# Feed-forward of a hybrid recurrent step: the sample tokens of two or three tile pairs at once

## The chip, the cores and the metric

The kernel runs on one core of a Trainium2 chip: TensorE (matrix products), VectorE and GpSimd (elementwise), ScalarE (activations and copies), SyncE (here the queue that issues transfers), all beside each other. The metric is the device time of one execution in microseconds; the time that stands for a kernel is the median of its runs.

## The reference, cut to what matters

One layer of a decoder trunk for 512 prompt tokens and 8 sample sequences of 8 tokens each (576 token columns: `T`, of which `TP` = 512 are the prompt's). Four token mixers come first; the change is in what follows them:

```
xn2 = rmsnorm(x, norm2_w)
up, buf_ffn = causal_dwconv(xn2 @ ffn_up, buf_ffn, ffn_conv_w, ffn_conv_b)   # width 3; 1024 -> 5632
gate_h, val_h = split(up, 2)
x = x + (gelu(gate_h) * val_h) @ ffn_down                                    # 2816 -> 1024
```

```
def causal_dwconv(u, buf, w, b):
    full = concatenate([buf, u], axis=1)       # buf: the 2 inputs before the sequence
    out = b
    for j in range(3):
        out = out + full[:, j:j + n] * w[j]
    return out, full[:, n:]                    # the last 2 inputs are an output as well
```

For the prompt `buf` is zero; each sample sequence has its own.

## The kernel before

Channels lie on the 128 partitions and tokens along the columns. All products are float32 products made of three: a matrix is split into a high part (`whi`, `ah`: a copy by ScalarE with rounding) and a low part (`wlo`, `al`: the difference, by VectorE or GpSimd), and high x high, high x low and low x high are added up in PSUM.

In the feed-forward stage (`tail`) the 44 column tiles of `ffn_up` are worked off in 22 pairs: tile i of the gate half with tile 22 + i of the value half. `K.pair` forms each pair's products by Strassen's scheme in Winograd's form, with seven products in place of eight. For them it needs sums of weight tiles (L253, `wc` in SBUF and `mx` in PSUM), and seven sides that are split (L246 on ScalarE, L247 on VectorE or GpSimd by the list `STRASSEN`; `wsp` holds five high and five low tiles). The matmuls of a pair are L262: 7 products x 4 tiles x 3. Sums read in between are copied by ScalarE (L286), and the results are joined by VectorE and multiplied with each token's factor `rbc` (L677, L679, and GpSimd's L680) into `raw`, one 128 x 576 tile for each half.

`conv_tiles` then convolves each `raw` with `dwconv`. The prompt's 512 columns are accumulated in PSUM (`mx`): the last tap with the bias by ScalarE (L545), two taps by VectorE (L549). The samples' 64 columns are accumulated in SBUF (`accs`): ScalarE (L546), two short taps on VectorE (L556) and, by GpSimd, what the earlier inputs bring into the first two sums (L558, prepared once in `hist`, L584 to L592). GpSimd copies the last inputs aside for the state output (`fcs`, L686). The loop over the pairs takes gelu of the gate half and multiplies it with the value half, for the prompt and for the samples apart (L701, L702), and splits the joint tile `gl` into `ah` and `al` (L169, L170).

The pairs come in three chunks of 8, 7 and 7 (`CHUNKS`). After each chunk its rows of `ffn_down` are multiplied (L223 to L225, eight column tiles, two halves of 288 columns each, the second with the samples) and added to `x1` (L692). The last chunk's products are followed by the final norm and the outputs.

Nothing in this order is written by hand for an engine: a scheduler puts each engine's instructions into a queue by priorities and its own estimates when the kernel is built, so products with `ffn_down` and the next pair's weights can stand between each other. A queue runs in order.

## Time and profile before

| what | value |
|---|---|
| median of 3 runs | 1712.4 us (1711.94 to 1730.63) |
| span of the profiled execution | 1708.0 us |
| matmul busy, share of the span | 1623.3 us, 95% |
| VectorE busy | 1188.4 us, 70% |
| ScalarE busy | 694.8 us, 41% |
| GpSimd busy | 794.3 us, 47% |
| mean granted TensorE clock | 0.968 of full speed |

The span runs from the first to the last instruction of one execution; the time of a run is 4.4 us longer at the median, for what lies around it. Busy shares are means over stages that differ: the mixers fill most of the span, the stage with `ffn_up` and `ffn_down` lies from about 1276 to 1680 us. A matmul's recorded duration overlaps the next one's.

### The profile page before, as it was taken

How to read it: one execution, taken by the hardware profiler on the slowest of the kernel's cores; microseconds unless marked ns; L12 is line 12 of the kernel's file. 1: busy time of each engine (PE TensorE's matmuls, PEld its weight loads, DVE VectorE, ACT ScalarE, POOL GpSimd, SP SyncE). 2: the span in 40 equal slices, each digit the busy share in tenths (PEclk: the TensorE clock that was granted, in tenths of full speed). 3: DMA queues.
4: the chain of work that ended last, by engine and by line, in shares of the span. 5: the costliest groups of instructions: out<-in, count | busy, mean ns of one | idle time of the engine just before them, and what ended most of it. 6: DMA issues, size and time to landing. Idle time of an engine off the chain costs nothing. (4 is left out here: it accounts for less than half of the span.)

```text
span 1708.0 us, 32814 instructions
## 1 busy us (share of the span) xinstructions
PE 1623.3 (95%) x12200; PEld 1471.7 (86%) x12200; DVE 1188.4 (70%) x2584; ACT 694.8 (41%) x1489; POOL 794.3 (47%) x1013
## 2 busy tenths in 40 slices
PE   6989999999999998999999989999999999999997
PEld 5988888888888898878888888888998999989897
DVE  7888888777584288534338754686479965975985
ACT  6333323334332335323335443332356643653653
POOL 4645433435331356212235562275676734743750
PEclk9999889799899999989999999999999999999999
DMA  7545543453362456332336563665432332232232
GB/s 201 143 122 142 148 118 95 128 139 102 114 197 74 111 156 164 103 101 74 95 96 194 152 174 104 199 181 166 117 90 79 96 99 75 78 97 75 87 106 71
DMA packets 356452, 207.62 MB, mean 122 GB/s; under 512 B 110884, under 2 KB 328357, under 8 KB 356293
## 3 DMA queue, kind: packets, MB, share of 16 engines
q1 hardware_dynamic: 356293, 205.53, 43.0%
q8 instruction: 96, 1.57, 0.4%
q14 instruction: 63, 0.52, 0.1%
HBM read 151.54 MB, written 53.02 MB: 120 GB/s over the span
## 5 line engine op out<-in xcount | busy, mean ns | idle before, releaser
L223 PE MATMUL dn<-xh,whi 128*128 128x288 f32 x1392 | 429.3, 309 | 4.6 <-ACT st L414 1.9
L224 PE MATMUL dn<-xl,whi 128*128 128x288 f32 x1392 | 427.6, 307 | 2.0 <-DVE xl L170 1.7
L225 PE MATMUL dn<-xh,wlo 128*128 128x288 f32 x1392 | 427.2, 307 | 0.0
L223 PEld LDWEIGHTS dn<-xh,whi 128*128 128x128 f32 x1392 | 269.9, 194 | 19.4 <-issue 8.0
L224 PEld LDWEIGHTS dn<-xl,whi 128*128 128x128 f32 x1392 | 269.8, 194 | 14.6 <-issue 8.4
L225 PEld LDWEIGHTS dn<-xh,wlo 128*128 128x128 f32 x1392 | 270.1, 194 | 12.0 <-issue 7.8
L169 ACT CAST whi<-wraw 128x512 fp32r<-128x512 f32 (+1 forms) x278 | 173.5, 628 | 218.6 <-PE dn L224 209.6
L170 POOL TENSOR_TENSOR wlo<-wraw,whi 128x512 fp32r<-128x512 f32 x92 | 129.4, 1407 | 202.1 <-ACT whi L169 194.3
L170 DVE TENSOR_TENSOR wlo<-wraw,whi 128x512 fp32r<-128x512 f32 (+1 forms) x186 | 152.3, 819 | 72.1 <-ACT whi L169 60.8
L262 PE MATMUL dn<-big,whi 128*128 128x288 f32 x528 | 108.7, 298 | 8.7 <-ACT su L286 2.8
L247 POOL TENSOR_TENSOR wlo<-wraw,whi 128x512 fp32r<-128x512 f32 x66 | 90.1, 1372 | 48.1 <-ACT whi L246 48.0
L262 PE MATMUL dn<-xh,whi 128*128 128x288 f32 x352 | 104.8, 299 | 4.6 <-ACT whi L246 4.1
L223 PE MATMUL dn<-yh,whi 128*128 128x288 f32 x352 | 104.8, 304 | 3.0 <-ACT yh L166 1.9
L262 PE MATMUL dn<-xh,wlo 128*128 128x288 f32 x352 | 103.5, 298 | 4.4 <-POOL wlo L247 4.4
L224 PE MATMUL dn<-yl,whi 128*128 128x288 f32 x352 | 105.4, 300 | 1.1 <-DVE yl L167 1.1
L225 PE MATMUL dn<-yh,wlo 128*128 128x288 f32 x352 | 105.0, 299 | 0.0
L262 PE MATMUL dn<-xl,whi 128*128 128x288 f32 x352 | 103.5, 295 | 0.0
L223 PE MATMUL dn<-ah,whi 128*128 128x288 f32 (+2 forms) x324 | 95.1, 298 | 1.5 <-ACT ah L169 1.5
L224 PE MATMUL dn<-al,whi 128*128 128x288 f32 (+2 forms) x324 | 95.5, 296 | 0.6 <-DVE al L170 0.6
L262 PEld LDWEIGHTS dn<-big,whi 128*128 128x128 f32 x528 | 84.3, 188 | 12.5 <-ACT su L286 4.5
L225 PE MATMUL dn<-ah,wlo 128*128 128x288 f32 (+2 forms) x324 | 95.0, 295 | 0.0
L262 PE MATMUL dn<-big,wlo 128*128 128x288 f32 x264 | 77.7, 295 | 0.1
(743 smaller groups left out, 4093.1 us busy)
## 6 DMA issues: line engine op xcount, KB each, us to landing
wraw<-w_in SPq DMA_DIRECT2D x55, 512.0 KB
wraw<-ffn_up SPq DMA_DIRECT2D x44, 512.0 KB
wraw<-w_merge SPq DMA_DIRECT2D x32, 512.0 KB
gate<-gst SPq DMA_DIRECT2D x32, 288.0 KB
g<-gate SPq DMA_DIRECT2D x32, 288.0 KB
wraw<-ffn_down SPq DMA_DIRECT2D x16, 448.0 KB
pd_hg<-st SPq DMA_DIRECT2D x16, 288.0 KB
wraw<-w_br_ssd SPq DMA_DIRECT2D x8, 512.0 KB
```

The costliest lines, as they stand in the source:

```text
L169: nc.scalar.copy(out=hi, in_=src)
L170: lo_engine.tensor_tensor(out=lo, in0=src, in1=hi.bitcast(F32), op=ALU.subtract)
L223: nc.tensor.matmul(ps, wh, xh[k][:, sl], start=k == 0, stop=False)
L224: nc.tensor.matmul(ps, wh, xl[k][:, sl], start=False, stop=False)
L225: nc.tensor.matmul(ps, wl, xh[k][:, sl], start=False, stop=k == len(wt) - 1)
L247: TT[eng](out=lo, in0=src, in1=hi.bitcast(F32), op=ALU.subtract)
L262: nc.tensor.matmul(ps, wt[:, k], x, start=start and k == 0 and i == 0, stop=k == n - 1 and i == 2, skip_group_check=not start)
```

## The change

The samples leave `dwconv`. `conv_tiles` lets GpSimd copy the last two prompt columns and the 64 sample columns of each `raw` aside into `rs` (66 columns). The pairs of a chunk are grouped (3, 3, 2 or 3, 2, 2), and behind each group a new function `samples` does the convolution, gelu, product and split for its 4 or 6 tiles at once, with the taps' columns, the bias and the history put in a fitting order once, before the stage (`cols`, `hists`). `ah` and `al` become one tile each with room for eight. For the first two chunks the first two column tiles of `ffn_down` are taken together: first half of both, then second half of both. Comments were dropped from the whole file as well.

```
-def dwconv(K, acc, raw, hist, taps, w, bias, small, split=None):
+def dwconv(K, acc, raw, hist, taps, w, bias, small):
...
-    if split is None:
-        nc.scalar.activation(acc, raw, AF.Identity, bias=bias, scale=w(n - 1))
-    else:
-        nc.scalar.activation(acc, raw[:, :TP], AF.Identity, bias=bias, scale=w(n - 1))
-        nc.scalar.activation(split, raw[:, TP:], AF.Identity, bias=bias, scale=w(n - 1))
+    nc.scalar.activation(acc, raw if hist is not None else raw[:, :TP], AF.Identity, bias=bias, scale=w(n - 1))
     for j in range(n - 1):
...
+    if hist is None:
+        return
...
-    if split is not None:
-        for j in range(n - 1):
-            sh = n - 1 - j
-            nc.vector.scalar_tensor_tensor(out=av[:, :, sh:], in0=rv[:, :, :LS - sh], scalar=w(j), in1=av[:, :, sh:],
-                                           op0=ALU.mult, op1=ALU.add)
-        nc.gpsimd.tensor_tensor(out=av[:, :, :n - 1], in0=av[:, :, :n - 1], in1=hist, op=ALU.add)
-        return
...
     mul(hist[:, :, 1], hist[:, :, 1], w0)
...
+    hists = x1p.tile([P, 22, 2, NS, 2], F32, name="fhs")
+    cols = x1p.tile([P, 4, 22, 2], F32, name="fcol")
+    for h in range(2):
+        hc = slice(22 * h, 22 * h + 22)
+        for e_ in range(2):
+            nc.gpsimd.tensor_copy(out=hists[:, :, h, :, e_], in_=hist[:, :, e_, hc].rearrange("p b c -> p c b"))
+        for j in range(4):
+            nc.gpsimd.tensor_copy(out=cols[:, j, :, h], in_=K.vcs("ffn_conv_w", 44 * j, 44)[:, hc] if j < 3 else K.vcs("ffn_conv_b", 0, 44)[:, hc])
...
+    GROUPS = {8: (3, 3, 2), 7: (3, 2, 2)}
+
+    def conv_tiles(rs, *ms):
...
-        for m, raw in zip(ms, raws):
-            acc = K.ps(of="c"), fp.tile([P, T - TP], F32, tag="accs", bufs=3, name=K.n("accs"))
-            nc.gpsimd.tensor_copy(out=cs[:, :, :, m], in_=raw[:, TP - 2:].rearrange("p (b e) -> p b e", e=2)[:, 0::4, :])
-            dwconv(K, acc[0], raw, hist[:, :, :, m], 3, lambda j: K.vc("ffn_conv_w", j * 44 + m), K.vc("ffn_conv_b", m), fp, acc[1])
+        for h, (m, raw) in enumerate(zip(ms, raws)):
+            acc = K.ps(of="c")
+            nc.gpsimd.tensor_copy(out=rs[:, h], in_=raw[:, TP - 2:])
+            dwconv(K, acc, raw, None, 3, lambda j: K.vc("ffn_conv_w", j * 44 + m), K.vc("ffn_conv_b", m), fp)
             out.append(acc)
         return out
 
+    def samples(c, rs, ah, al):
...
+        n = rs.shape[1]
+        N = 2 * n
+        GT = nc.gpsimd.tensor_tensor
+        TT = nc.vector.tensor_tensor
+        r = rs.rearrange("p i h t -> p (i h) t")
+        for h in range(2):
+            m = slice(22 * h + c, 22 * h + c + n)
+            nc.gpsimd.tensor_copy(out=cs[:, 0, :, m].rearrange("p e c -> p c e"), in_=rs[:, :, h, :2])
+            for e_ in range(2):
+                nc.gpsimd.tensor_copy(out=cs[:, 1:, e_, m].rearrange("p b c -> p c b"), in_=rs[:, :, h, 2 + LS - 2 + e_::LS])
+        w = [cols[:, j, c:c + n].rearrange("p c h -> p (c h)").unsqueeze(2) for j in range(4)]
+        acc = fp.tile([P, 6, T - TP], F32, tag="sacc", bufs=2, name=K.n("sacc"))[:, :N]
+        GT(out=acc, in0=r[:, :, 2:], in1=w[2].to_broadcast([P, N, T - TP]), op=ALU.mult)
+        GT(out=acc, in0=acc, in1=w[3].to_broadcast([P, N, T - TP]), op=ALU.add)
+        av = acc.rearrange("p m (b t) -> p m b t", t=LS)
+        rv = r[:, :, 2:].rearrange("p m (b t) -> p m b t", t=LS)
+        ts = []
+        for j, sh in ((1, 1), (0, 2)):
+            t = fp.tile([P, 6, NS, LS], F32, tag="stap", bufs=2, name=K.n("stap"))[:, :N, :, :LS - sh]
+            TT(out=t, in0=rv[:, :, :, :LS - sh], in1=w[j].unsqueeze(3).to_broadcast([P, N, NS, LS - sh]), op=ALU.mult)
+            ts.append((sh, t))
+        GT(out=av[:, :, :, :2], in0=av[:, :, :, :2], in1=hists[:, c:c + n].rearrange("p c h b e -> p (c h) b e"), op=ALU.add)
+        for sh, t in ts:
+            TT(out=av[:, :, :, sh:], in0=av[:, :, :, sh:], in1=t, op=ALU.add)
+        a = acc.rearrange("p (i h) t -> p i h t", h=2)
+        g = fp.tile([P, 3, T - TP], F32, tag="sgl", bufs=2, name=K.n("sgl"))[:, :n]
+        nc.scalar.activation(g, a[:, :, 0], AF.Gelu_apprx_tanh)
+        TT(out=g, in0=g, in1=a[:, :, 1], op=ALU.mult)
+        K.split(ah, al, g, nc.vector)
+
...
     for k0, n in CHUNKS:
-        ah = [fp.tile([P, T], F32R, tag=f"ah{k}", name=K.n("ah")) for k in range(n)]
-        al = [fp.tile([P, T], F32R, tag=f"al{k}", name=K.n("al")) for k in range(n)]
-        for i in range(n):
-            accs = conv_tiles(k0 + i, 22 + k0 + i)
-            gl = fp.tile([P, T], F32, tag="gl", bufs=2, name=K.n("gl"))
-            for sl, a0, a1 in zip((slice(0, TP), slice(TP, T)), *accs):
-                nc.scalar.activation(gl[:, sl], a0, AF.Gelu_apprx_tanh)
-                nc.vector.tensor_tensor(out=gl[:, sl], in0=a1, in1=gl[:, sl], op=ALU.mult)
-            K.split(ah[i], al[i], gl, nc.vector)
...
+        hl = [fp.tile([P, 8, T], F32R, tag=t, name=K.n(t))[:, :n] for t in ("ah", "al")]
+        ah, al = ([t[:, k] for k in range(n)] for t in hl)
+        i = 0
+        for size in GROUPS[n]:
+            rs = fp.tile([P, 3, 2, T - TP + 2], F32, tag="rs", bufs=2, name=K.n("rs"))[:, :size]
+            for a in range(size):
+                a0, a1 = conv_tiles(rs[:, a], k0 + i, 22 + k0 + i)
+                gl = fp.tile([P, TP], F32, tag="gl", bufs=2, name=K.n("gl"))
+                nc.scalar.activation(gl, a0, AF.Gelu_apprx_tanh)
+                nc.vector.tensor_tensor(out=gl, in0=a1, in1=gl, op=ALU.mult)
+                K.split(ah[i][:, :TP], al[i][:, :TP], gl, nc.vector)
+                i += 1
+            samples(k0 + i - size, rs, *(t[:, i - size:i, TP:] for t in hl))
         if k0 + n < 22:
-            for m in K.dense(down, k0, n, 0, 8, ah, al, evac):
...
+            wt = [K.weights(down, k0, n, m * P) for m in range(2)]
+            for j in range(2):
+                for m in range(2):
+                    K.part(wt[m], slice(j * H2, (j + 1) * H2), ah, al, m, evac)
+            for m in K.dense(down, k0, n, 2 * P, 6, ah, al, lambda m, sl, ps: evac(m + 2, sl, ps)):
                 pass
```

## Rows read from the trace of the kernel before

**Rows 1.** The page: span, and busy time of each engine.

```profile
span 1708.0 us, 32814 instructions
...
PE 1623.3 (95%) x12200; PEld 1471.7 (86%) x12200; DVE 1188.4 (70%) x2584; ACT 694.8 (41%) x1489; POOL 794.3 (47%) x1013
```

**Rows 2.** Stretches: length, busy us (x instructions) of PE, PEld, DVE, ACT, POOL, clock, DMA.

```profile
1275.70:1377.40 101.70, 96.00 (x682) 91.28 (x682) 100.31 (x180) 66.37 (x140) 72.82 (x84) 1.00 0.30 85
1377.40:1427.80 50.40, 50.40 (x382) 50.40 (x381) 24.99 (x46) 14.43 (x25) 11.02 (x12) 1.00 0.28 81
1427.80:1516.00 88.20, 82.17 (x602) 80.03 (x601) 80.46 (x138) 54.13 (x111) 62.50 (x71) 1.00 0.30 88
...
1560.80:1650.70 89.90, 83.86 (x615) 81.66 (x614) 82.21 (x142) 55.72 (x114) 63.99 (x74) 1.00 0.30 86
...
1295.00:1377.40 82.40, 79.08 (x568) 75.75 (x567) 81.86 (x149) 55.22 (x116) 60.77 (x76) 1.00 0.32 92
1441.00:1516.00 75.00, 69.84 (x511) 67.94 (x511) 72.84 (x127) 48.06 (x99) 54.67 (x64) 1.00 0.31 89
1574.00:1650.00 76.00, 70.83 (x519) 68.86 (x518) 73.74 (x129) 49.05 (x101) 55.40 (x66) 1.00 0.30 88
```

**Rows 3.** Who waited for whom from 1275 to 1651 us: total, times, longest.

```profile
ACT whi L246 <- DVE mx L253: 20.3, 18, 2.2
...
ACT whi L246 <- DVE wc L253: 15.1, 14, 1.8
...
PE dn L262 <- ACT whi L246: 5.9, 10, 1.0
...
PE dn L262 <- POOL wlo L247: 4.4, 5, 1.2
```

**Rows 4.** One pair in order of time, VectorE, and a row of GpSimd: start, us.

```profile
1331.92 0.67 DVE L702 TENSOR_TENSOR gl<-mx,gl 128x512 f32<-128x512 f32 x1
...
1335.17 0.56 DVE L556 SCALAR_TENSOR_TENSOR accs<-raw,vecs,accs 128x48 f32<-128x48 f32 x2
...
1335.76 2.57 POOL L247 TENSOR_TENSOR wlo<-wraw,whi 128x512 fp32r<-128x512 f32 x2 [0.27 <-ACT whi L246]
...
1336.91 1.49 DVE L556 SCALAR_TENSOR_TENSOR accs<-raw,vecs,accs 128x56 f32<-128x56 f32 x2
...
1343.82 0.68 DVE L702 TENSOR_TENSOR gl<-mx,gl 128x512 f32<-128x512 f32 x1
```

**Rows 5.** VectorE's taps and the samples' product by line: duration min/median/max in ns.

```profile
L549 DVE SCALAR_TENSOR_TENSOR mx<-raw,vecs,mx x88: 735/742/754, 1297.5 to 1655.6; 128x510 f32<-128x510 f32 x44, 128x511 f32<-128x511 f32 x44
...
L556 DVE SCALAR_TENSOR_TENSOR accs<-raw,vecs,accs x88: 252/378/1327, 1299.6 to 1654.6; 128x48 f32<-128x48 f32 x44, 128x56 f32<-128x56 f32 x44
...
L702 DVE TENSOR_TENSOR gl<-accs,gl x22: 208/433/1310, 1306.6 to 1655.4; 128x64 f32<-128x64 f32 x22
```

**Rows 6.** Groups of VectorE's instructions: busy us, mean ns of one, idle before.

```profile
L556 DVE SCALAR_TENSOR_TENSOR accs<-raw,vecs,accs 128x48 f32<-128x48 f32 (+1 forms) x88 | 49.5, 598 | 0.0
...
L679 DVE TENSOR_TENSOR raw<-su,dn 128x288 f32<-128x288 f32 x44 | 19.4, 442 | 0.0
...
L702 DVE TENSOR_TENSOR gl<-accs,gl 128x64 f32<-128x64 f32 x22 | 11.8, 537 | 0.0
```

**Rows 7.** GpSimd's instructions by line: duration min/median/max in ns.

```profile
L686 POOL COPY fcs<-raw x44: 217/220/760, 1298.5 to 1650.6; 128x18 f32<-128x18 f32 x44
...
L558 POOL TENSOR_TENSOR accs<-accs,fhist x44: 223/244/814, 1303.7 to 1655.0; 128x16 f32<-128x16 f32 x44
...
L680 POOL TENSOR_TENSOR raw<-raw,rbc x66: 798/811/1254, 1295.7 to 1652.5; 128x288 f32<-128x288 f32 x66
...
L247 POOL TENSOR_TENSOR wlo<-wraw,whi x66: 1266/1297/3109, 1265.3 to 1640.4; 128x512 fp32r<-128x512 f32 x66
```

**Rows 8.** GpSimd in order of time ahead of the stage: start, us, [idle before].

```profile
1239.22 1.40 POOL L592 TENSOR_TENSOR fhist<-fhist,fht 128x352 f32<-128x352 f32 x1
...
1258.40 1.60 POOL L654 TENSOR_TENSOR sqacc<-sqacc,sq 128x576 f32<-128x576 f32 x1 [3.83 <-ACT sq L653]
```

More of the change, by code (lines that the diff above doesn't have):

```diff
@@ L550, in dwconv @@
                                        op0=ALU.mult, op1=ALU.add)
+    if hist is None:
+        return
     rv = raw[:, TP:].rearrange("p (b t) -> p b t", b=NS)
-    av = (acc[:, TP:] if split is None else split).rearrange("p (b t) -> p b t", b=NS)
-    if split is not None:
-        for j in range(n - 1):
-            sh = n - 1 - j
-            nc.vector.scalar_tensor_tensor(out=av[:, :, sh:], in0=rv[:, :, :LS - sh], scalar=w(j), in1=av[:, :, sh:],
-                                           op0=ALU.mult, op1=ALU.add)
-        nc.gpsimd.tensor_tensor(out=av[:, :, :n - 1], in0=av[:, :, :n - 1], in1=hist, op=ALU.add)
-        return
+    av = acc[:, TP:].rearrange("p (b t) -> p b t", b=NS)
     ext = small.tile([P, NS, LS + n - 1], F32, tag="ext", name=K.n("ext"))
@@ L668, in tail @@
     CHUNKS = ((0, 8), (8, 7), (15, 7))
-    def conv_tiles(*ms):
+    GROUPS = {8: (3, 3, 2), 7: (3, 2, 2)}
+    def conv_tiles(rs, *ms):
         raws = [fp.tile([P, T], F32, tag="raw", bufs=3, name=K.n("raw")) for _ in ms]
```

## The prediction

> **What bounds the kernel now.** I read the page's sums first, then the feed-forward stage in stretches, then who waits for whom, and last one pair in order of time. The page says that TensorE is busy for 95% of a span of 1708.0 us [rows 1]. That number hides the stage that the change touches, because matmuls overlap each other in the record; the count of matmuls is the better measure. While the first chunk is multiplied with ffn_down, 382 matmuls pass in 50.40 us without a gap, 0.132 us each; that is TensorE's own pace here, at a granted clock of 1.00 (the 2.4 GHz level) in every row of the group [rows 2]. One column tile pair is 7 products x 4 tiles x 3 matmuls = 84 matmuls, so 11.1 us if TensorE sets the pace. In the stretches with ffn_up it doesn't: 682 matmuls take 101.70 us where 90.0 would do, 602 take 88.20 for 79.4, 615 take 89.90 for 81.2 [rows 2]. The loss is 11.7 + 8.8 + 8.7 = 29.2 us, and it is all that any change to this stage can win: 1.7% of the time.
>
> In the middle of these stretches VectorE is the full engine: busy 81.86 of 82.40 us, 72.84 of 75.00, 73.74 of 76.00 [rows 2]. Those three middles hold 568, 511 and 519 matmuls, 6.8, 6.1 and 6.2 pairs, at 12.1 to 12.3 us a pair, and lose 7.4 + 7.5 + 7.5 = 22.4 of the 29.2 us. The rest is the start of each chunk, where no sample work has begun. TensorE's direct waits are short and name ScalarE's and GpSimd's halves of the weights (5.9 and 4.4 us) [rows 3]; but ScalarE waits for VectorE's weight sums (20.3 and 15.1 us) [rows 3], so the chain leads back to VectorE. One steady pair shows it: the gated product of the prompt comes at 1331.92 and again at 1343.82, 11.90 us apart [rows 4].
>
> **What is removed on VectorE.** Per pair the four short taps of the samples (L556) and the samples' gate product (L702 on accs) go: 88 and 22 instructions that occupy 49.5 and 11.8 us [rows 6], 61.3 us or 2.8 us a pair. That is far more than their 48 to 64 elements ask for: the taps run from 252 to 1327 ns and the product from 208 to 1310, while the prompt's taps, ten times longer, stay between 735 and 754 [rows 5]. The steady pair shows the reason: two short taps that begin at 1336.91 last 1.49 us, and GpSimd's two weight parts, begun at 1335.76, end at 1338.33 [rows 4]; the pair of taps begun at 1335.17, before them, takes 0.56. Instructions with both inputs in SBUF wait there for a GpSimd instruction to end; the prompt's taps have one input in PSUM and don't. At their minimum the 110 instructions would cost 88 x 0.252 + 22 x 0.208 = 26.8 us; the other 34.5 us are such waits, 0.31 us each. The low part shrinks from 576 to 512 columns, some 0.07 us a pair.
>
> The Trainium skill, "GPSIMD Engine Reference", section "Key points", says that GpSimd shares its SBUF interfaces with VectorE and contends with VectorE instructions that have two SBUF inputs. The rows agree, and the rule speaks against the change as much as for it, since all six new VectorE instructions are of that kind; this is the second rival below. The skill's "Perfetto Trace Analysis", section "Optimizing Scalar/DVE Operations", gives some 60 ns of fixed cost to a VectorE instruction on SBUF; 110 instructions less 54 would by that alone be an estimate of 3.4 us, where the rows above give a multiple.
>
> **What is added on VectorE.** A group (four of three pairs, five of two) has six instructions: two tap products, two sums, the gate product, the low part. From 442 ns at 288 elements [rows 6] and 742 at 510 [rows 5], an element costs 1.35 ns. A group of three: 2 x 0.51 (336 elements) + 2 x 0.44 (288) + 2 x 0.31 (192) = 2.5 us; of two, with 224, 192 and 128: 2 x (0.36 + 0.31 + 0.23) = 1.8. Sum 4 x 2.5 + 5 x 1.8 = 19 us, 0.9 a pair. That is without waits; with 0.31 us on each of the 54 it is 17 more, 0.8 a pair. VectorE's 11.9 to 12.1 us a pair (its busy time in the three middles by their pairs) become 11.9 - 2.8 - 0.1 + 0.9 = 9.9 at best, and 10.7 with waits on the new ones. A last term isn't visible: the weight sums wc and mx and the low part have two SBUF inputs too (L253, L170), so a GpSimd instruction that delayed a tap may now delay them. At 0.31 us for each of three or four that is about 1 us a pair, 11.7 in all. Bounds 9.9 to 11.7, TensorE's pace 11.1. I take 10.7, nearest to the row in which short instructions wait as often as they do now.
>
> **GpSimd.** It loses two state copies (220 ns) and two history sums (244 ns) a pair [rows 7], 44 x 0.46 = 20 us at the medians. It gains two copies aside of 66 columns a pair: between 0.22 us (18 elements) and 0.81 (288, two inputs) [rows 7], I take 0.28, near the short one, 12 us in all. A group gains six state copies (0.22 each), a product and a sum with broadcast columns, and a history sum. From 811 ns at 288 and 1297 at 512 elements [rows 7], 384 elements cost 1.02 us, 256 cost 0.74, the history sum 0.3 to 0.4: 1.3 + 2.0 + 0.4 = 3.8 us for three pairs, 3.1 for two, together 4 x 3.8 + 5 x 3.1 = 31 us. Net 31 + 12 - 20 = +23 us, 1 us a pair on an engine that is busy 54.67 us in 6.1 pairs, 9.0 each [rows 2]: it goes to about 10 of 11.5. It is not the bound by its sum, but its queue is in order, and behind a block of 3 to 4 us stand the four low parts of the weights that it makes for each pair and that TensorE reads, and the row scaling that ScalarE's convolution reads. What covers such a block is the depth of five weight buffers, less than one pair's seven sides.
>
> **What costs nothing or little.** The history and column copies before the stage are 12 short GpSimd instructions, 4 x some 0.6 + 8 x 0.22 = 4 us, in the stretch in which the history is made (its last instruction begins at 1239.22); GpSimd stands idle 3.83 us before 1258.40 there [rows 8], which hides them. If that cover were gone they would delay the row factors by up to 4 us, once. ScalarE drops 66 instructions and gains 18; it is busy 55.22 of 82.40 us [rows 2] and gains room. The larger tiles ah and al change no order, since the next chunk's first write waits for the last ffn_down tile in either form. The samples now finish after the prompt; for two chunks four half tiles of ffn_down come in an order in which two prompt halves, 6.3 or 5.5 us of TensorE, go first; for the last chunk it is one, 21 x 0.132 = 2.8 us. A sample chain of six VectorE instructions (1.8 us), two on ScalarE and GpSimd's 3.1 us overlaps with the prompt's own. I take 2 us of exposed tail in all, bounds 0 and 6. Holding two weight tiles at once leaves one of five buffers for the third; it fills while the fourth half runs, 3.2 us against 1 to 2 us of split. No DMA moves.
>
> **The sum.** If VectorE needs 10.7 us on average but 2 us more in one pair of two or three, and GpSimd's block falls in the same pair, TensorE's 11.1 won't be held throughout; I take 11.4 to 11.5 a pair, which gives back about 14 of the 22.4 us. Less 2 us of tail: -12 us. The profiled execution has 1708.0 us of span beside a median of 1712.4, 4.4 us outside that stay: 1696 of span, **1700 us**.
>
> **The rivals.** (a) All comes back: VectorE falls to 9.9 us, blocks and tails are hidden. Then 22.4 us less: 1690. For it: the short taps' waits are the odd part of the rows. Against it: GpSimd at 90%. (b) The waits only move: VectorE stays at 11.7 us a pair, 0.2 to 0.5 us less over 19 pairs, some 6 us, less a tail of 2 to 6: -3 us, 1709, with 1706 to 1714 about it. For it: GpSimd stays as busy as before, and VectorE's next instruction with two SBUF inputs meets it in the place of the tap. It is also the case in which the change doesn't do what it says. The page of the Trainium skill on GpSimd, named above, states its rule without regard to an instruction's length, which would be this case. (c) Slower: GpSimd's blocks stand in front of the weights' low parts. All nine uncovered cost 31 us; against a gain of 12 the change loses from 39% uncovered, and at two thirds it is -12 + 20 = +8: 1721, at worst 1731. For it: TensorE waits for GpSimd's low parts already [rows 3]. Against it: five buffers let these parts be made ahead of their product, and the two kinds of wait on weights in the whole stage sum to no more than 10.3 us [rows 3].
>
> **How the numbers follow.** Forecast 0.50 (1694 to 1706), (a) 0.17 (1686 to 1694), (b) 0.18 (1706 to 1714), (c) 0.15 (1714 to 1731). The range 1688 to 1717 leaves out most of (c) and the lowest end of (a), under 2 in 10. Two per cent, about what a measurement here can tell from no change, is 34 us, more than the whole loss of the stage; faster by that 0.02, slower 0.02, within 0.96.
>
> **What would show it.** Right: the middles of the three ffn_up stretches hold a matmul per 0.135 us or so, VectorE's share falls to about 93%, GpSimd's rises; taps at L549 unchanged. Wrong: long wc, mx or low parts (b); TensorE's waits for GpSimd's low parts of 15 us and more (c); idle between the last pair and the second half of the first ffn_down tiles (tail); or an order of engine queues so different that pairs no longer run alike, which no row of the kernel before can exclude.

## The result, and the profile after

The changed kernel takes 1731.4 us at the median (1725.5 to 1746.9), beside 1714.4 us of the kernel before in the same series: a ratio of 1.0105, 95% interval 1.0081 to 1.0129. The change was forecast to gain 12 us and costs 17. Its profiled execution has a span of 1725.2 us:

```profile
span 1725.2 us, 32713 instructions
...
PE 1627.0 (94%) x12200; PEld 1478.0 (86%) x12200; DVE 1182.1 (69%) x2528; ACT 683.3 (40%) x1441; POOL 817.2 (47%) x1062
```

By the page VectorE's sum is a little down and GpSimd's 23 us up, against [rows 1]. Where the time went is in the stretches of the feed-forward stage, which answer to [rows 2] (length, then busy us of PE, PEld, DVE, ACT, POOL, then the granted clock):

```profile
1277.50:1387.00 109.50, 98.08 (x688) 94.56 (x687) 98.42 (x160) 64.05 (x124) 80.33 (x93) 0.97 0.29 82
...
1436.90:1529.00 92.10, 83.15 (x604) 81.64 (x603) 79.07 (x123) 51.73 (x99) 64.50 (x81) 0.98 0.29 84
...
1576.50:1667.90 91.40, 83.60 (x619) 82.08 (x618) 78.09 (x124) 52.81 (x100) 67.16 (x83) 1.00 0.30 85
1297.00:1387.00 90.00, 80.88 (x572) 78.75 (x571) 79.76 (x129) 52.73 (x100) 68.27 (x85) 0.96 0.31 88
1450.40:1529.00 78.60, 71.74 (x520) 70.47 (x519) 72.44 (x114) 46.28 (x88) 57.85 (x76) 0.98 0.29 85
1588.80:1667.00 78.20, 71.28 (x528) 69.99 (x527) 70.18 (x113) 46.55 (x88) 58.83 (x77) 1.00 0.30 85
```

VectorE is busy 79.76 of 90.00, 72.44 of 78.60 and 70.18 of 78.20 us in the middles: 89 to 92%, where it was 97 to 99% [rows 2]. It got its room, and the matmuls still pass more slowly: 90.00 us for 572 is 0.157 us each, before it was 0.145. From the first pair's first matmul to the last pair's last the stage takes 390.6 us instead of 375.8. These 14.8 us are what there is to explain; the setup copies ahead of the stage and the work behind it cost nothing that shows (52.0 instead of 51.9 us for the product ahead of it, 57.1 instead of 56.6 behind). Another 1.8 us of the difference between the spans lie ahead of that product, where the change adds nothing.

Who waited for whom in the stage (us in total, times, longest), which answers to [rows 3]:

```profile
PE dn L262 <- DVE raw L681: 19.7, 13, 3.2
...
DVE wc L253 <- DMA wraw<-ffn_up: 17.7, 14, 2.9
...
PE dn L262 <- POOL wlo L247: 1.5, 3, 0.8
```

And two lines of the kernel before that [rows 3] doesn't have:

```profile
PE dn L262 <- ACT su L286: 2.8, 4, 1.1
PE dn L262 <- DVE raw L679: 2.7, 6, 0.6
```

Two waits are new in this size. TensorE waits 19.7 us for `raw`, a sum that VectorE reads from PSUM, 2.7 us before; and VectorE itself waits 17.7 us for weights, 5.2 us before. GpSimd's low parts, the fear of rival (c), fell from 4.4 to 1.5 us. VectorE's groups in the stage (busy us, mean ns, idle before), which answer to [rows 5, 6]:

```profile
L545 DVE SCALAR_TENSOR_TENSOR mx<-raw,vecs,mx 128x510 f32<-128x510 f32 x88 | 65.5, 746 | 1.7 <-ACT mx L542 1.1
...
L253 DVE TENSOR_TENSOR mx<-wraw 128x512 f32<-128x512 f32 x21 | 22.9, 1093 | 0.0
L170 DVE TENSOR_TENSOR al<-gl,ah 128x512 fp32r<-128x512 f32 x22 | 22.9, 1042 | 3.9 <-ACT ah L169 3.9
L253 DVE TENSOR_TENSOR wc<-wraw,wraw 128x512 f32<-128x512 f32 x21 | 22.4, 1064 | 17.7 <-DMA wraw<-ffn_up 17.7
...
L718 DVE TENSOR_TENSOR sacc<-sacc,stap 128x224 f32<-128x224 f32 (+3 forms) x18 | 11.4, 631 | 0.2
L714 DVE TENSOR_TENSOR stap<-rs,fcol 128x224 f32<-128x224 f32 (+3 forms) x18 | 10.3, 612 | 1.1 <-POOL rs L688 0.7
...
L170 DVE TENSOR_TENSOR al<-sgl,ah 128x128 fp32r<-128x128 f32 (+1 forms) x9 | 6.6, 738 | 0.0
L722 DVE TENSOR_TENSOR sgl<-sgl,sacc 128x128 f32<-128x128 f32 (+1 forms) x9 | 3.3, 362 | 0.4 <-ACT sgl L721 0.4
```

The same weight sums and low part in the kernel before:

```profile
L170 DVE TENSOR_TENSOR al<-gl,ah 128x576 fp32r<-128x576 f32 x22 | 18.8, 856 | 3.6 <-ACT ah L169 3.4
...
L253 DVE TENSOR_TENSOR mx<-wraw 128x512 f32<-128x512 f32 x21 | 17.2, 819 | 0.0
...
L253 DVE TENSOR_TENSOR wc<-wraw,wraw 128x512 f32<-128x512 f32 x21 | 15.3, 729 | 5.2 <-DMA wraw<-ffn_up 5.2
```

So of the 61.3 us taken from VectorE, 31.6 came back in the new instructions (10.3 + 11.4 + 6.6 + 3.3) and 16.9 as longer `wc`, `mx` and `al` (7.1 + 5.7 + 4.1); 12.8 us stayed away by these rows. All of VectorE's busy time in the stage fell by 8 us, from 310.8 to 302.6. The prompt's taps, with one input in PSUM, are unchanged at 746 ns.

**The pairs that carry a group are longer.** Chunk 2 from its second to its sixth pair, cut at every 84th matmul (the kernel before took 12.5, 11.3, 13.4, 12.0 and 13.9 us at these places, so its pairs weren't alike either):

```profile
1450.40:1462.30 11.90, 11.44 (x87) 11.21 (x86) 9.44 (x16) 7.01 (x13) 7.17 (x9) 1.00 0.31 90
1462.30:1474.30 12.00, 11.41 (x86) 11.18 (x85) 11.00 (x18) 7.45 (x14) 8.35 (x9) 1.00 0.31 88
1474.30:1488.40 14.10, 11.62 (x86) 11.21 (x85) 14.04 (x20) 7.64 (x14) 12.86 (x19) 1.00 0.26 76
1488.40:1503.40 15.00, 12.90 (x86) 12.70 (x85) 14.59 (x24) 8.20 (x16) 10.37 (x14) 0.89 0.25 72
1503.40:1516.00 12.60, 11.37 (x86) 11.17 (x85) 10.95 (x18) 7.62 (x14) 11.36 (x15) 1.00 0.26 78
```

The first two carry no group's work on VectorE: VectorE is busy 9.44 and 11.00 us, yet they take 11.9 and 12.0. The next two carry the group of three: VectorE is full (14.04 of 14.10), GpSimd busy 12.86 and 10.37 us instead of some 8. Over the stage, six pairs without a group's VectorE work take 71.5 us where the same places took 72.2 before; nine with it take 126.0 where 114.7 were taken; the other seven, first pairs and chunk ends, 4.1 us more. Sum: -0.7 + 11.3 + 4.1 = 14.7; of the 4.1 us, 3.0 fall at the end of chunk 2.

How a loss comes about, in order of time at the end of the fourth of these pairs:

```profile
1494.73 1.29 DVE L253 TENSOR_TENSOR wc<-wraw,wraw 128x512 f32<-128x512 f32 x1
...
1495.43 1.73 POOL L247 TENSOR_TENSOR wlo<-wraw,whi 128x512 fp32r<-128x512 f32 x1
...
1495.94 1.78 DVE L253 TENSOR_TENSOR mx<-wraw 128x512 f32<-128x512 f32 x1
...
1497.12 1.71 POOL L247 TENSOR_TENSOR wlo<-wc,whi 128x512 fp32r<-128x512 f32 x1
...
1498.29 0.44 DVE L681 TENSOR_TENSOR raw<-sp,dn 128x288 f32<-128x288 f32 x1
```

VectorE's two weight sums of the next pair run while GpSimd makes low parts and take 1.29 and 1.78 us where the shortest of their kind takes 0.69. Behind them in VectorE's queue stands `raw<-sp`, the result `out(0, 0)`, which frees the bank of `c`. The next pair's P7 is put into that bank, and in TensorE's queue, of both kernels, the first two matmuls of P7 stand ahead of the current pair's P3. TensorE's own rows show the gap (in brackets), and what follows it:

```profile
1498.88 0.50 PE L262 MATMUL dn<-big,whi 128*128 128x288 f32 x2 [2.10 <-DVE raw L681]
...
1499.91 0.44 PE L262 MATMUL dn<-xh,whi 128*128 128x288 f32 x1
1500.15 0.44 PE L262 MATMUL dn<-xl,whi 128*128 128x288 f32 x1
```

The matmuls then start 0.24 us apart instead of 0.13: the granted clock is at its lower level, as after a gap in chunk 1 too (first row; the second is the stretch behind it):

```profile
1342.60:1346.00 3.40, 3.31 (x14) 3.34 (x15) 2.83 (x5) 1.39 (x4) 1.87 (x4) 0.51 0.00 0
1346.00:1350.00 4.00, 4.00 (x32) 4.00 (x32) 3.29 (x5) 2.59 (x6) 1.82 (x2) 1.00 0.00 0
```

In 3.40 us at 0.51 pass 14 matmuls where 26 would at 0.132 us each: 1.6 us lost. The profiled execution after has four such stretches in the stage, the one before none; by an estimate from these counts about 6 of the 14.8 us are this.

### The profile page after: what moved, and what is told of

Read it like the earlier page. It is cut to its first block, busy times and chain, and to the rows that moved or that the text cites. A ratio compares the mean times of both kernels' runs of the same rounds, so it can differ in the third digit from the quotient of the medians.

```text
span 1725.2 us, 32713 instructions
## 1 busy us (share of the span) xinstructions
PE 1627.0 (94%) x12200; PEld 1478.0 (86%) x12200; DVE 1182.1 (69%) x2528; ACT 683.3 (40%) x1441; POOL 817.2 (47%) x1062
## 5 line engine op out<-in xcount | busy, mean ns | idle before, releaser
L223 PEld LDWEIGHTS dn<-xh,whi 128*128 128x128 f32 x1392 | 270.4, 194 | 19.5 <-issue 8.4
L224 PEld LDWEIGHTS dn<-xl,whi 128*128 128x128 f32 x1392 | 270.6, 194 | 14.4 <-issue 8.4
```

Of the source, the lines that this page charges most:

```text
L223: nc.tensor.matmul(ps, wh, xh[k][:, sl], start=k == 0, stop=False)
L224: nc.tensor.matmul(ps, wh, xl[k][:, sl], start=False, stop=False)
```

## The experiments

Ratios are to the kernel before on the same chip, with 95% intervals; "stage" is as above (375.8 us before, 390.6 after), from the run's profiled execution. That is one execution, and the times of one kernel's runs lie some 20 us apart, so a few microseconds of stage alone prove little.

**Is VectorE's sum the bound, and where do its waits go?**

e1, the changed kernel without the samples' feed-forward:

```
...
-            nc.gpsimd.tensor_copy(out=rs[:, h], in_=raw[:, TP - 2:])
...
         n = rs.shape[1]
-        N = 2 * n
...
-        K.split(ah, al, g, nc.vector)
+        nc.scalar.copy(out=ah, in_=zero[:, :n])
+        nc.scalar.copy(out=al, in_=zero[:, :n])
```

> The changed kernel with the samples' feed-forward left out: their columns of the split tiles are filled with zeros by ScalarE, and GpSimd's copies aside and all of the group's work are gone. Theory 1 (moved waits: VectorE's long instructions with two SBUF inputs, the weight sums wc and mx and the low part al, now meet GpSimd's low parts where the short taps did, and the sums that free PSUM for TensorE queue behind them): the low parts are still there, so wc and mx stay at a mean of 900 ns or more, TensorE still waits 8 us or more for VectorE's raw, and the time is 1712 to 1727. Rival 1 (the blocks of sample work on GpSimd do the harm): wc and mx under 800 ns, the pairs run at 11.1 to 11.5 us, time 1690 to 1705. Rival 2 (the new order of the first ffn_down tiles): 1712 or more, with the waits of wc and mx gone.

Measured 0.9972 (0.994 to 1.0004), stage 373.5. All of the samples' work gone, from VectorE, GpSimd and ScalarE, is worth 2 us of stage against the kernel before. The second to sixth pairs of the later chunks take 11.8 to 12.2 us. VectorE waits 23.3 us for weights.

e4, the kernel before without the short taps and the samples' gate product:

```
...
-            nc.vector.scalar_tensor_tensor(out=av[:, :, sh:], in0=rv[:, :, :LS - sh], scalar=w(j), in1=av[:, :, sh:],
-                                           op0=ALU.mult, op1=ALU.add)
...
+                if sl.start == 0:
                     nc.vector.tensor_tensor(out=gl[:, sl], in0=a1, in1=gl[:, sl], op=ALU.mult)
```

> The kernel before with the samples' two short taps per tile and their gate product on VectorE left out (the sample columns take the last tap, the history and gelu alone); everything else stays. 61 us of recorded VectorE time go. Theory 1: at least 12 us of waiting turn up in wc, mx and al instead, VectorE's total falls by 40 us or less, and the time falls by 10 us at most: 1704 to 1718. Rival (the short instructions were plain load): 1690 to 1700.

Measured 1.0011 (0.9981 to 1.0041), stage 382.1. Exactly the 110 instructions that the forecast set at 61.3 us are gone and nothing is put in their place, and nothing is gained. The lines show where the waits went:

```profile
L170 DVE TENSOR_TENSOR al<-gl,ah 128x576 fp32r<-128x576 f32 x21 | 25.9, 1233 | 3.1 <-ACT ah L169 3.1
L253 DVE TENSOR_TENSOR mx<-wraw 128x512 f32<-128x512 f32 x21 | 25.4, 1209 | 0.0
L253 DVE TENSOR_TENSOR wc<-wraw,wraw 128x512 f32<-128x512 f32 x21 | 22.7, 1082 | 19.4 <-DMA wraw<-ffn_up 19.3
```

The sums and the low part are 0.35 to 0.39 us longer each, and the idle time before `wc` went from 5.2 to 19.4 us. In [rows 4] the tap pair of 1.49 us ended when GpSimd's two parts ended; without the taps, it is the next instruction with two SBUF inputs that meets this end, as the longer rows say. TensorE's waits for `raw` are 10.1 us here (2.7 before), there are four stretches at half clock, and the stage is 6 us longer.

e11 puts idle short taps on top of the changed kernel, e9 makes every group a single pair:

```
...
+            for j in range(2):
+                sh = 2 - j
+                nc.vector.scalar_tensor_tensor(out=idle[:, h, :, sh:], in0=rv[:, :, :LS - sh], scalar=K.vc("ffn_conv_w", j * 44 + m),
+                                               in1=idle[:, h, :, sh:], op0=ALU.mult, op1=ALU.add)
...
+                nc.vector.tensor_tensor(out=idle[:, 2], in0=idle[:, 1], in1=idle[:, 0], op=ALU.add)
```
```
-    GROUPS = {8: (3, 3, 2), 7: (3, 2, 2)}
+    GROUPS = {8: (1,) * 8, 7: (1,) * 7}
```

> The changed kernel plus four short taps a pair and one short sum on VectorE, of the shapes that the change removed, whose results nothing uses: 110 instructions more, 27 us at their minima and 61 us as they ran in the kernel before. Theory (moved waits): the added instructions take waits that the weight sums had, and the order on VectorE goes back to nearly that of before; not slower than the changed kernel, ratio 1.000 to 1.010, TensorE's waits for raw under 15 us. Rival (VectorE's work counts): VectorE is busy 89 to 92% of the middles at 13 us a pair; 1.2 to 2.8 us more a pair fills it, 10 to 30 us more on the stage, ratio 1.016 to 1.03.

> The changed kernel with the samples of each single pair handled by themselves (22 groups of one instead of nine of two or three): 22 x 6 = 132 short instructions on VectorE instead of 54, and GpSimd's share cut into 22 short blocks. Theory (moved waits: short instructions with two SBUF inputs take the waits for GpSimd, and without them the weight sums take them right ahead of a read that TensorE waits for): more short instructions take more of the waits, TensorE's waits for raw fall from 19.7 us to under 12, ratio to the kernel before 0.999 to 1.007, not slower than the changed kernel (1.0105). Rival A (work counts: 78 more instructions on VectorE, some 117 more on GpSimd at about 0.22 us, 26 us more on an engine that is busy 229 to 249 us): slower than the changed kernel, 1.013 to 1.02. Rival B (the length of GpSimd's blocks): the loss is gone, 0.992 to 0.999.

Measured 1.0178 (1.0139 to 1.0217) for e11 and 1.0128 (1.0092 to 1.0164) for e9, stages 406.6 and 397.9. The theory that short instructions shelter the weight sums fell: TensorE's waits for `raw` are small in e11 (4.3 us), but its waits for ScalarE's copies `su` rise to 12.7 us and the stage is 16 us longer than that of the changed kernel. Work put on VectorE costs, though work taken off it gives nothing.

**The order of ffn_down.** e2, the changed kernel with the old order of the first two tiles:

```
-            wt = [K.weights(down, k0, n, m * P) for m in range(2)]
...
+            for m in K.dense(down, k0, n, 0, 8, ah, al, evac):
```

> The changed kernel with the first two ffn_down tiles of a chunk in the old order, one tile after the other. Theory 1 and rival 1: within 4 us of the changed kernel, 1727 to 1736 (a later second half could even cost 1 to 3 us). Rival 2: 6 us or more come back, 1725 or less.

Measured 1.0062 (1.0037 to 1.0087), stage 390.3. The stage is that of the changed kernel, and so are the 19.5 us of waits for `raw`; the ratio lies 0.4% lower, with intervals that overlap, so that a small part for this order is not excluded.

**GpSimd's share.** e3 gives the samples' last tap and bias to ScalarE, tile by tile; e14 gives it a group's six state copies; e8 does GpSimd's product and sum twice:

```
-        GT(out=acc, in0=r[:, :, 2:], in1=w[2].to_broadcast([P, N, T - TP]), op=ALU.mult)
-        GT(out=acc, in0=acc, in1=w[3].to_broadcast([P, N, T - TP]), op=ALU.add)
+        for i in range(n):
+            for h in range(2):
+                nc.scalar.activation(acc[:, 2 * i + h], rs[:, i, h, 2:], AF.Identity, bias=cols[:, 3, c + i, h:h + 1], scale=cols[:, 2, c + i, h:h + 1])
```
```
-            nc.gpsimd.tensor_copy(out=cs[:, 0, :, m].rearrange("p e c -> p c e"), in_=rs[:, :, h, :2])
+            nc.scalar.copy(out=cs[:, 0, :, m].rearrange("p e c -> p c e"), in_=rs[:, :, h, :2])
...
```
```
...
+        GT(out=acc2, in0=r[:, :, 2:], in1=w[2].to_broadcast([P, N, T - TP]), op=ALU.mult)
+        GT(out=acc2, in0=acc2, in1=w[3].to_broadcast([P, N, T - TP]), op=ALU.add)
```

> The changed kernel with the samples' last tap and bias back on ScalarE, 44 instructions of 64 columns, in place of GpSimd's 18 product and sum instructions (13 us of GpSimd's work). Theory 1: wc and mx still at 950 ns or more, time 1724 to 1734. Rival 1: half of the loss or more comes back, 1722 or less.

> The changed kernel with the six state copies of a group on ScalarE instead of GpSimd; nothing else. Theory (the bunch): GpSimd's block falls from 4.4 to 5.0 us to some 3 us in its pair, and as with the last tap and the bias on ScalarE (ratio 0.996) most of the loss is gone: pairs that carry the block 12 to 13 us instead of 13.2 to 16.0, stage 374 to 382, ratio 0.996 to 1.003. Rival (it is not the block but where the weight sums fall in VectorE's queue): as the changed kernel, 1.007 to 1.013, stage 386 to 393.

> The changed kernel with GpSimd's product and sum of a group done twice (the first result is not used): 13 us more GpSimd work in nine blocks. Taking these blocks away gave back some 20 us. If the blocks act by making VectorE's weight sums late, and with them the read of b that P4 waits for: 6 to 20 us slower than the changed kernel, 1737 to 1752, TensorE's waits for raw 22 us or more. If the queue order alone made the difference: within 5 us of the changed kernel, either way.

Measured: e3 0.9959 (0.9927 to 0.999), stage 373.5; e14 1.0076 (1.0045 to 1.0108), stage 388.1; e8 1.0092 (1.0051 to 1.0134), stage 393.1. e3 and e14 take nearly the same from GpSimd (its 235.4 us of busy time in the stage become 222.2 and 224.5), and one ends the loss while the other keeps most of it. Twice the product and sum adds 10 us on GpSimd and 2.5 us to the stage. So GpSimd's sum, and the mere length of its block, don't set the loss. What else e3 changes is that its ScalarE work is spread, 0.9 us in every pair, and stands elsewhere in the built order; these two weren't separated. VectorE's busy time doesn't decide it either: 302.6 us become 292 in e3 and 309 in e14, but 298 in e8.

**The read that TensorE waits for.** e10 lets ScalarE copy `c` out of PSUM, so that its bank comes free without VectorE; e6, e5 and e7 split the product P2 in halves, the second after P5 and ahead of `out(1, 1)` and `out(0, 0)`, on the changed kernel, the one before, and e3:

```
-        out(0, 0, p1, c)
+        v = self.scr.tile([P, H2], F32, tag="sc", bufs=2, name=self.n("sc"))
...
+            nc.scalar.copy(out=v, in_=c)
+        out(0, 0, p1, v)
```
```
...
-        product("P2", c, True)
-        out(0, 0, p1, c)
+        product("P2", c, True, range(n // 2))
         product("P5", a, False)
         u5 = seen("su5")
+        product("P2", c, True, range(n // 2, n))
         out(1, 1, u5, b)
+        out(0, 0, p1, c)
```

> The changed kernel in which ScalarE copies the sum of P2 (c) out of PSUM and VectorE adds from that copy, so that c's bank comes free without VectorE. In the queue of TensorE the first two matmuls of the next pair's P7 stand ahead of P3, and they need that bank. Theory (that bank is the deadline): TensorE's waits for raw fall from 19.7 us to under 4, no or one stretch at half clock, stage 372 to 381 us against 390.6, ratio 0.995 to 1.003. Rival (the waits for raw are only the place where a loss shows that has its cause elsewhere, in VectorE's or GpSimd's sum of work): the loss comes out at another wait, stage 387 to 394, ratio 1.007 to 1.014; the added copy on ScalarE (22 x 0.5 us) and a sum with two SBUF inputs on VectorE would only add to it.

> The changed kernel with the same move of half of P2. Theory 2: TensorE's waits for VectorE's raw (19.7 us in the changed kernel) fall under 9 us, fewer clock drops in the stage, 1700 to 1716. Rival (work of VectorE or GpSimd sets the pair): 1725 to 1734.

> The kernel before with the second half of product P2 moved between P5 and P3, and the sum that reads b issued ahead of the one that reads c; nothing else. In the records so far TensorE stops at two places of a pair: before P3, which must wait for ScalarE's copy of P5's sum (about 0.55 us), and before P4, which must wait until VectorE has read b. Theory 2 (deadlines: what counts is how late these two reads come, not VectorE's total): P2's half covers the copy and gives the read of b 0.8 us more; half a microsecond a pair and more comes back, 1699 to 1708. Rival (VectorE's sum of work sets the pair, as the prediction had it): 1711 to 1718.

> The changed kernel with the last tap and bias of the samples on ScalarE and with the move of half of P2: both remedies. Theory 2: the waits of TensorE for VectorE's raw under 4 us, 1694 to 1706, the fastest so far. Rival: not faster than the one with ScalarE alone, 1707 to 1716.

Measured: e10 1.0091 (1.0056 to 1.0125), stage 387.9; e6 0.9993 (0.9962 to 1.0025), 376.6; e5 0.9901 (0.9872 to 0.993), 366.7; e7 0.9969 (0.9937 to 1.0002), 372.0. In e10 the waits for `raw` are nearly gone and the loss is not:

```profile
DVE wc L253 <- DMA wraw<-ffn_up: 20.5, 14, 3.9
...
PE dn L262 <- POOL wlo L247: 6.2, 10, 1.1
...
PE dn L262 <- DVE raw L684: 2.9, 3, 1.0
```

So the 19.7 us were the place at which the loss showed rather than its cause; but e10 also adds 22 copies on ScalarE and gives that sum two SBUF inputs, so some of its loss may be its own. e6 points the same way: its waits for `raw` are 1.4 us, and it is still slower than e5. The split (which also covers ScalarE's copy of P5's sum, see e13 below) gains 1% on either kernel: 0.9901 to 1 before, 0.9993 to 1.0105 after. Between the two kernels with it the ratio is 0.9993 / 0.9901 = 1.009: the change costs the same with the deadline eased. e5, the kernel before with the split alone, beats both kernels; combining it with e3 did not add up.

**The bunch.** e13, one group a chunk:

```
-    GROUPS = {8: (3, 3, 2), 7: (3, 2, 2)}
+    GROUPS = {8: (8,), 7: (7,)}
...
-            rs = fp.tile([P, 3, 2, T - TP + 2], F32, tag="rs", bufs=2, name=K.n("rs"))[:, :size]
+            rs = fp.tile([P, 8, 2, T - TP + 2], F32, tag="rs", bufs=1, name=K.n("rs"))[:, :size]
...
```

The tiles of a group have room for eight pairs, but one buffer each instead of two.

> The changed kernel with one group a chunk (8, 7 and 7 pairs) instead of three, so that no pair before the last of a chunk carries sample work on VectorE or GpSimd but the two copies aside. Theory (the bunch: a group's work falls into one pair and fills GpSimd there, 13.6 to 14.1 us of pairs of 13.2 to 16.0 us, and VectorE in the next): the pairs inside the chunks run at 11.2 to 12.6 us throughout, mean about 12.1 as without any samples, and the whole loss stands at the ends of the chunks, where a chain of some 12 us less 5.5 to 6.3 us of prompt halves is left open: stage 380 to 395. Rival (the waits of the weight sums for GpSimd's weight parts, whatever the samples do): pairs of 13 to 16 us stay in the chunks, mean 12.8 or more, and the ends come on top: 395 to 410.

Measured 1.0206 (1.0164 to 1.0248), stage 392.2. With no group's work inside a chunk the pairs are alike:

```profile
1461.20:1473.00 11.80, 11.35 (x86) 11.12 (x85) 9.17 (x16) 7.00 (x13) 7.12 (x8) 1.00 0.32 91
1473.00:1485.10 12.10, 11.46 (x87) 11.23 (x86) 10.94 (x18) 7.46 (x14) 8.35 (x9) 1.00 0.31 87
1485.10:1497.10 12.00, 11.41 (x86) 11.18 (x86) 10.91 (x18) 7.53 (x14) 8.34 (x9) 1.00 0.31 89
```

The long pairs are those that carry a group: shown. The bunch is paid for at the chunk's end instead: the two stretches from a chunk's last pair to the next chunk take 74.8 and 69.1 us where 62.2 and 57.5 were, with TensorE's waits there 18.2 us and the clock at half in them for 10.2 us each, and the work behind the stage takes 70.0 us instead of 57.1. How much of that the single buffers add wasn't tried.

The same rows show the second thing: these pairs hold at 12.0 us with VectorE busy 10.9 of it. In the third of them VectorE waits once, for a load of raw weights, and TensorE waits once, for ScalarE's copy of P5's sum, ahead of P3:

```profile
1486.84 1.29 POOL L247 TENSOR_TENSOR wlo<-wraw,whi 128x512 fp32r<-128x512 f32 x1 [0.60 <-ACT whi L246]
...
1488.16 2.68 SPq L240 DMA_DIRECT2D wraw<-ffn_up  x2
...
1492.02 0.99 DVE L253 TENSOR_TENSOR wc<-wraw,wraw 128x512 f32<-128x512 f32 x1 [1.05 <-DMA wraw<-ffn_up]
```
```profile
1495.62 0.40 PE L262 MATMUL dn<-xh,whi 128*128 128x288 f32 x1 [0.59 <-ACT su L286]
```

The first of the two loads goes out behind GpSimd's low part that reads the same buffer last (1486.84 + 1.29 = 1488.13), and VectorE stands idle 1.05 us until it lands. But no matmul of this pair waits for weights. At the copy the matmuls stand 0.88 us apart instead of 0.13; that is 0.75 of the 0.9 us by which the pair is longer than 84 matmuls. Every pair of 11.8 to 12.2 us from the second to the fifth of the later chunks, here and in e1, has this stop, 0.6 to 0.9 us long, and no other of its size. Whether the load or the copy holds such a pair is settled by e6 above, which has the five weight buffers and the samples' work, but half of P2 between P5 and P3. Its second and third pairs of chunk 2, freed ones, run at TensorE's pace without a stop:

```profile
1448.90:1460.10 11.20, 11.20 (x87) 11.20 (x86) 8.10 (x14) 6.78 (x13) 9.14 (x11) 1.00 0.33 96
1460.10:1471.20 11.10, 11.10 (x86) 11.10 (x86) 10.44 (x18) 8.07 (x16) 7.54 (x9) 1.00 0.32 94
```

So do those of chunk 3, and the same four pairs in e7. What held the freed pairs at 12.0 us is the copy that nothing covers, not VectorE's sum, and not the load.

**The weights' buffers.** e15 and e16 give P4 a weight buffer of its own beside the five, in the changed kernel and the one before; e17 does it in the kernel of e1, e18 in that of e3. e12 is e4 with the split P2:

```
-            hi = self.wsp.tile([P, 4, P], F32R, tag="whi", name=self.n("whi"))[:, :n]
...
+            pool, tg = (self.wsp2, "2") if name in self.deep else (self.wsp, "")
+            hi = pool.tile([P, 4, P], F32R, tag="whi" + tg, name=self.n("whi"))[:, :n]
...
+    K.wsp2, K.deep = cfn.enter_context(tc.tile_pool(name="wsp2", bufs=1)), ("P4",)
```

> The changed kernel with one weight buffer more in the feed-forward stage (P4's two parts have a buffer of their own beside the five). Theory (the weights' supply has too little slack for a block of 4 to 5 us): the block is spread over neighbouring pairs, TensorE's waits fall from 30.7 to about 20 us, stage 372 to 382, ratio 0.995 to 1.003. Rival (the bunch fills an engine, or the waits for raw don't depend on the weights' buffers): 1.006 to 1.013.

> The kernel before with the same extra weight buffer. If the supply of weights (few buffers) keeps its pairs at 11.9 us and above: 0.988 to 0.996, pairs towards 11.3 us. If VectorE's sum keeps them there, as the prediction had it: no change, 0.998 to 1.003.

> The changed kernel without the samples' feed-forward (their columns of the hidden layer are zero, no copies aside), as in the run that gave 0.997 with steady pairs of 12.0 to 12.2 us, and with P4's own weight buffer. Theory (a pair freed of sample work is held at 12 us by the supply of weights, not by VectorE): steady pairs 11.1 to 11.4 us, TensorE's own pace, stage 358 to 367, ratio 0.984 to 0.993. Rival (VectorE and its waits for GpSimd hold it at 12): pairs of 12, ratio 0.994 to 1.001.

> The changed kernel with P4's own weight buffer and with the samples' last tap and bias on ScalarE. Theory (two causes that add: the block in one pair, and the supply of weights in the others): pairs without a block 11.1 to 11.4 us, with one 12 to 14, less some 3 us that the first pair loses with the extra buffer; stage 364 to 371, ratio 0.989 to 0.996. Rival (they don't add): as the better of the two alone or worse, 0.996 to 1.004.

> The kernel before with the product P2 split in halves (the second half after P5, which alone gave 0.990), and without the four short taps and the samples' gate product on VectorE: the samples' outputs leave these terms out. Theory (moved waits; VectorE's sum is not the bound): nothing more is gained by leaving out 61 us of VectorE's busy time, ratio 0.988 to 0.998. Rival (VectorE's sum is a bound once TensorE's waits for raw are gone): 0.975 to 0.985, a stage of 347 to 360 us against 366.7.

Measured: e15 1.0073 (1.0041 to 1.0106), stage 382.0; e16 1.0002 (0.9975 to 1.0028), 377.0; e17 0.9941 (0.9904 to 0.9978), 365.4; e18 0.9999 (0.997 to 1.0028), 378.1; e12 0.9952 (0.9924 to 0.998), 374.8. Read e1, e16 and e17 together with the kernel before: the samples' work away, 373.5; a buffer more, 377.0; both, 365.4, from 375.8. Each alone gives nothing that the ratio can tell, both give 10 us of stage. In e17 the pairs do reach TensorE's pace (second to fifth of chunk 2):

```profile
1457.30:1468.50 11.20, 11.20 (x87) 11.20 (x86) 7.90 (x15) 6.93 (x13) 7.64 (x8) 1.00 0.29 80
1468.50:1479.90 11.40, 11.32 (x86) 11.12 (x86) 10.77 (x18) 7.69 (x15) 7.30 (x7) 1.00 0.37 107
1479.90:1494.60 14.70, 12.83 (x85) 12.60 (x85) 10.85 (x20) 7.71 (x15) 8.09 (x8) 0.88 0.26 74
1494.60:1505.70 11.10, 11.10 (x86) 11.10 (x85) 10.04 (x16) 7.54 (x14) 8.51 (x8) 1.00 0.35 97
```

but one of 14.7 us stands between them, with a wait of 1.9 us for that copy and half clock in it, and the ratio came out above the 0.984 to 0.993 expected, at the edge of the rival's range. In the pairs of 11.1 to 11.4 us the stop ahead of P3 is gone as well; with one buffer more the built order of TensorE's queue differs, and whether the buffer acts by it or by the supply of weights wasn't separated. VectorE waits 28.8 us for weights in e17, more than in e1, so that wait alone doesn't tell the pace. e18's two remedies did not add; e15's ratio lies 0.3% under that of the changed kernel, within the noise, and its pairs that carry a group still take up to 15.3 us. In e12, leaving the 61.3 us out made the best kernel, e5, no faster; the ratio is 0.5% higher, with intervals that just overlap.

## Why the prediction was wrong

**What bounds the kernel.** That VectorE is full in the middles was read rightly [rows 2], and e16 agrees: a sixth weight buffer alone gives nothing. But "full" held waits, and behind it stood a second limit at almost the same pace. A pair freed of sample work takes 12.0 us (e1, e13), because TensorE stops ahead of P3 for ScalarE's copy of P5's sum, 0.6 to 0.9 us a pair; where half of P2 covers it, freed pairs take 11.1 to 11.2 (e6). The forecast put "TensorE's pace 11.1" next, the matmuls alone, and this stop at nothing, although TensorE's waits for `su` stood in the trace before (2.8 us, four times).

**The step that failed is the sum**: "I take 11.4 to 11.5 a pair, which gives back about 14 of the 22.4 us". The middles hold 12.4 to 13.2 us a pair (90.00, 78.60 and 78.20 us for 572, 520 and 528 matmuls). The sum averaged VectorE's work over pairs, and put TensorE's matmuls behind it. Freed pairs gave 0.7 us in all; pairs that carry a group, for which "2 us more in one pair of two or three" was allowed within that mean, cost 11.3 us more than before. VectorE's mean came out at 11.2 to 11.7 us a pair in the middles, not 10.7, and in the single pairs of chunk 2 above it runs from 9.4 to 14.6.

**Removed on VectorE**: 61.3 us was right as a row and wrong as a price. 34.5 us of it were rightly called waits for GpSimd, but these end when GpSimd's part ends, whoever meets them; e4 agrees, with these instructions left out and nothing else changed. **Added on VectorE**: 31.6 us, within the 19 to 36 of the text. **The last term**, moved waits at about 1 us a pair, "isn't visible" in the text and was not taken: it is 16.9 us over 22 pairs, 0.8 a pair, near the 1 us of the text. The Trainium skill, "GPSIMD Engine Reference", section "Key points", has such contention for VectorE's instructions with two SBUF inputs; the rows agree, `wc` from 729 to 1064 ns and the taps with a PSUM input unchanged at 746.

**GpSimd**: +23 us forecast for the stage, with 4 more for the setup. The page has +22.9 in all (794.3 to 817.2), of which 6.0 lie ahead of the stage and 16.9 from its start on; near enough, and not the cause in itself (e8). **What costs nothing**: the setup copies were hidden. The tail, 2 us with bounds 0 and 6: seven first pairs and chunk ends cost 4.1.

**The rivals.** (b) named the mechanism, moved waits, but gave it a gain of 3 us. (c) had the sign, with 1721 and at worst 1731, by a wait that did not come: TensorE's waits for GpSimd's low parts fell. The clock stood in no step; four stretches at half clock cost about 6 us by the estimate above. The last sentence of the text, an order "so different that pairs no longer run alike", is the nearest to what came, though the pairs before weren't alike either (11.3 to 13.9 us in chunk 2).

**Still open**: which part of a group's work makes its pairs long, since e3 and e14, with nearly the same relief of GpSimd, disagree (in e14 the second pair that carries a group in the later chunks is down to 12.3 us, but the first takes 14.4 and the chunks' ends grow); and what makes the slow pairs of e17. More buffers for the raw weights were not tried.

## What to carry to other kernels

A queue that is 99% busy with instructions that wait for another engine does not come free by removing the waiting ones; take the forecast's new pace from the next engine's own stops in its rows, not from its count of instructions alone. An idle engine is no limit by itself: VectorE stood idle for weights in pairs where TensorE waited for something else. When small work is batched over several iterations, cost the iteration that carries the batch, not the mean: the freed iterations gain only as far as the next limit, the carrying one pays in full, and a gap on TensorE can cost again at half clock.

## What the hardware showed beyond that

A GpSimd instruction that runs beside a VectorE instruction with two SBUF inputs can be longer itself: the low part took 1.73 us beside `wc` and `mx` (timeline above), where its median before was 1297 ns [rows 7].

After an idle of 2.10 us on TensorE the clock stood at its lower level (1.2 of 2.4 GHz) for some 3.4 us; gaps of 0.90 and 1.59 us earlier in the same chunk were not followed by that. The length of the gap alone doesn't decide it: after idles of 2.09 us (until 1445.81) and 2.08 us (until 1637.29) of the same execution the clock stayed up, and in e4 it fell after one of 1.85. In e13 it fell during a wait of 5.25 us that ended at 1397.09 and stayed low for 10.2 us, in which only 20 matmuls ran:

```profile
1395.70:1405.90 10.20, 5.68 (x20) 4.99 (x21) 6.23 (x9) 1.86 (x3) 0.14 (x1) 0.50 0.00 0
```
